# The last 512 columns of five weight stages, token-major like the rest

## The chip, the cores and the metric

The kernel runs on one core of a Trainium2 chip. The metric is the time of one execution on the device in microseconds (us). Three runs of the kernel before gave 1565.44 to 1566.68, median 1566.22. The engines are named as the profile names them: PE is TensorE (PEld its weight loads), DVE VectorE, ACT ScalarE, POOL GpSimd, and SP the queue from which nearly all loads are issued.

## What is computed

One layer over 256 tokens of width 2048, all in float32.

```
xn = rms_norm(x, norm_mix_g)
proj = xn @ w_in                        # 2048 -> 11264
u_s5, u_lru, q, k, v, gate_logits = split(proj)
g_s5, g_lru, g_attn = split(sigmoid(gate_logits + b_gate))      # 2048 each
y_s5   = s5_branch(u_s5)                # scan, gelu, gated by w_glu; width 1024
y_lru  = rglru_branch(u_lru)            # convolution, gates, scan; width 1024
y_attn = stick_breaking_attention(q, k, v)                      # 8 heads of 128
merged = g_s5*(y_s5 @ w_br_s5) + g_lru*(y_lru @ w_br_lru) + g_attn*(y_attn @ w_br_attn)
h = x + merged @ w_out                  # 2048 -> 2048
hidden = relu(rms_norm(h, norm_mlp_g) @ w_up) ** 2              # 2048 -> 8192
out = rms_norm(h + hidden @ w_down, final_norm_g)               # 8192 -> 2048
```

## The kernel before, in words

The work is one long stream of weights. Each weight matrix is cut into chunks of 512 output columns, and each chunk into units of two k-tiles (256 rows, 512 KB). Three buffers hold raw units, and three hold split units. A unit is loaded from SP's queue (L118), then split into two float32r parts: ACT casts it to `hi` (L134), and DVE subtracts to get `lo` (L135). The activations are split in the same way into a high and a low part, and each product is three matmuls: high by high, high by low, low by high. `next_unit` loads up to three units ahead and splits up to two ahead of the unit in use.

A chunk is computed in one of two ways. `chunk` (L196 to L198, tiles named mm_) holds 128 columns of the weights still and streams 256 tokens, so the result has channels on partitions: 12 matmuls of 256 columns for each k-tile. `chunk_tok` (L212 to L214, tiles named mt_) holds 128 tokens still and streams the 512 weight columns, so the result has tokens on partitions: 6 matmuls of 512 columns for each k-tile. Channel-major is the form that the next product needs as its input. A token-major result that the next product reads is brought over by `blocks`: 16 DVE transposes (L677), each a set of 32 by 32 blocks.

The stages, in order: parts of w_in; for lru and attn four times a gate chunk of w_in and a branch chunk; the same for s5, in the order g0, g1, w_glu twice, b0, g2, b1, b2, g3, b3; w_out (four chunks); then four rounds of w_up (four chunks of 512) and w_down (four chunks). In the gates, branches, w_out and each round of w_up the first three chunks are token-major and the fourth is channel-major. All of w_down is token-major.

Side work is written as generators. `later` puts one in a list with a rate, and `pump`, called after each unit's matmuls, takes that many steps from each. The S5 scan runs so beside the gates and attention. `split_tok` transposes 512 columns of the merged branches and splits them for w_out; `residual` transposes 512 columns of the residual `h_tok` into `hT` and splits them for w_up; `norm2` brings the last 512 columns of `hT` back to tokens with 16 transposes (L933), sums squares (L305, L309, L312) and ends in the PE matmuls `ps_n` (L923) and a few DVE steps; `hidden` transposes a chunk of relu(w_up), squares it on ACT and POOL (L987, L988) and splits it (L991) for w_down. Engines take their instructions in the order in which they are written, apart from small moves by a scheduler.

The lines that the change touches: in `gates` and `branch` the fourth chunk has its own code (L339, L702, L715 to L718). After the last s5 branch it is split at once (L852, L853). After w_out's fourth chunk the residual is added channel-major (L913) and split (L891, L892). After w_up's fourth chunk four instructions for each half make the split parts (L1013 to L1016). The residual input `xres` is loaded on ACT's queue (L878).

## Time and profile before

| | |
|---|---|
| median of three runs | 1566.22 us |
| profiled execution | 1565.52 us, its span 1563.8 us |
| PE busy | 1520.8 us (97%), 8430 matmuls |
| DVE busy | 1162.6 us (74%) |
| ACT busy | 807.9 us (52%) |
| POOL busy | 219.0 us (14%) |
| DMA | 291.78 MB, mean 187 GB/s |

The profile is one execution on the chip. Busy is the time in which an engine worked. Matmuls overlap each other in it, so the length of a stage and not the sum of its matmuls tells its cost. A row of the timeline shows start, duration, engine, line, operation, what it writes and reads, how many were merged, and in brackets the idle time before it with what ended that. A row of the stretches shows from:to, the length, the busy time of each engine with its count of instructions, the granted TensorE clock (1.00 is full), the busy share of the DMA engines and GB/s.

### The profile page before, as it was taken

To read this page: it belongs to the slowest core of one execution; us is meant where nothing else is said; L and a number is where in the kernel's file an instruction comes from. 1 tells how busy PE (TensorE), PEld (TensorE's weight loads), DVE (VectorE), ACT (ScalarE), POOL (GpSimd) and SP (SyncE) were. 2 spreads that over 40 slices of the span, in tenths; PEclk is the share of its full clock that TensorE was granted. 3 is DMA by queue.
4 is the path that set the end of the run, shared out by engine and by line. 5 is a ranking of instruction groups with operands and counts; after the bars stand their busy time and mean duration, and the time that the engine had idled before them with its cause. 6 is when DMAs were issued, how large, how long until landed. Compare 5 with 4: busy or idle time off the path is not lost.

```text
span 1563.8 us, 21927 instructions
## 1 busy us (share of the span) xinstructions
PE 1520.8 (97%) x8430; PEld 1316.4 (84%) x8430; DVE 1162.6 (74%) x1417; ACT 807.9 (52%) x976; POOL 219.0 (14%) x172
## 2 busy tenths in 40 slices
PE   9899999989999999999999999999999999999997
PEld 9897789978877788988889888888988898888986
DVE  5887998878979899578698895558655685558755
ACT  7468555486756555543444544344433444344443
POOL 5301113112112322101000010000100000000111
PEclk9999999999999999999999999999999999999999
DMA  9555665545536565655756556555566566655554
GB/s 282 156 169 172 188 197 174 176 135 168 178 115 199 172 188 176 205 192 167 279 191 194 183 167 197 194 193 191 189 194 196 189 190 192 196 190 192 191 196 148
DMA packets 88491, 291.78 MB, mean 187 GB/s; under 512 B 12738, under 2 KB 16962, under 8 KB 88130
## 3 DMA queue, kind: packets, MB, share of 16 engines
q1 hardware_dynamic: 87954, 287.14, 57.2%
q10 hardware_dynamic: 432, 3.24, 0.6%
q8 instruction: 66, 1.08, 0.3%
q14 instruction: 39, 0.32, 0.1%
HBM read 281.95 MB, written 2.10 MB: 182 GB/s over the span
## 4 chain that ended last, share of the span: by engine, by line
PE 80%; DVE 11%; ACT 4%; issue 3%; DMA 1%; DVEq 0%; ACTq 0%
PE mt_w_down L212 7%; PE mt_w_down L213 7%; PE mt_w_down L214 7%; PE mm_w_in L198 5%; PE mm_w_in L196 5%; PE mt_w_up L214 5%; PE mm_w_in L197 5%; PE mt_w_up L213 5%; PE mt_w_up L212 5%; DVE lo L135 4%; PE mt_w_in L213 3%; PE mt_w_in L214 3%; PE mt_w_in L212 3%; PE mm_w_up L198 2%; PE mm_w_up L197 2%
## 5 line engine op out<-in xcount | busy, mean ns | idle before, releaser
L135 DVE TENSOR_TENSOR lo<-raw,hi 128x1024 fp32r<-128x1024 f32 (+1 forms) x521 | 660.9, 1272 | 327.6 <-ACT hi L134 323.0
L134 ACT CAST hi<-raw 128x1024 fp32r<-128x1024 f32 (+1 forms) x521 | 545.3, 1049 | 661.2 <-PE mt_w_down L214 197.6
L198 PE MATMUL mm_w_in<-xhi,lo 128*128 128x256 f32 x704 | 202.1, 288 | 7.3 <-DVE lo L135 7.3
L196 PE MATMUL mm_w_in<-xhi,hi 128*128 128x256 f32 x704 | 202.4, 288 | 1.8 <-DVE rs L297 1.2
L213 PE MATMUL mt_w_down<-lo,hd_hi 128*128 128x512 f32 (+1 forms) x528 | 202.1, 383 | 0.0
L212 PE MATMUL mt_w_down<-hi,hd_hi 128*128 128x512 f32 (+1 forms) x528 | 202.1, 383 | 0.0
L214 PE MATMUL mt_w_down<-hi,hd_lo 128*128 128x512 f32 (+1 forms) x528 | 202.0, 383 | 0.0
L197 PE MATMUL mm_w_in<-xlo,hi 128*128 128x256 f32 x704 | 201.3, 286 | 0.0
L213 PE MATMUL mt_w_up<-lo,hhi 128*128 128x512 f32 x384 | 150.0, 391 | 2.5 <-DVE lo L135 2.5
L214 PE MATMUL mt_w_up<-hi,hlo 128*128 128x512 f32 x384 | 149.5, 389 | 0.0
L212 PE MATMUL mt_w_up<-hi,hhi 128*128 128x512 f32 x384 | 149.4, 389 | 0.0
L213 PE MATMUL mt_w_in<-lo,xhi 128*128 128x512 f32 x352 | 140.8, 400 | 7.5 <-DVE lo L135 7.3
L212 PE MATMUL mt_w_in<-hi,xhi 128*128 128x512 f32 x352 | 141.4, 403 | 3.9 <-ACT hi L134 3.9
L198 PEld LDWEIGHTS mm_w_in<-xhi,lo 128*128 128x128 f32 x704 | 136.9, 195 | 9.5 <-DVE lo L135 9.1
L196 PEld LDWEIGHTS mm_w_in<-xhi,hi 128*128 128x128 f32 x704 | 137.3, 195 | 4.1 <-issue 2.6
L214 PE MATMUL mt_w_in<-hi,xlo 128*128 128x512 f32 x352 | 139.4, 396 | 0.0
L197 PEld LDWEIGHTS mm_w_in<-xlo,hi 128*128 128x128 f32 x704 | 137.3, 195 | 0.2
L214 PEld LDWEIGHTS mt_w_down<-hi,hd_lo 128*128 128x128 f32 x528 | 99.2, 188 | 19.4
L212 PEld LDWEIGHTS mt_w_down<-hi,hd_hi 128*128 128x128 f32 x528 | 99.2, 188 | 19.3
L213 PEld LDWEIGHTS mt_w_down<-lo,hd_hi 128*128 128x128 f32 x528 | 99.2, 188 | 19.2
L988 POOL TENSOR_TENSOR reluT<-reluT 128x1024 f32<-128x1024 f32 x12 | 23.8, 1984 | 642.9 <-ACT hd_hi L987 519.5
L213 PEld LDWEIGHTS mt_w_up<-lo,hhi 128*128 128x128 f32 x384 | 72.1, 188 | 19.3 <-DVE lo L135 4.5
(328 smaller groups left out, 2600.0 us busy)
## 6 DMA issues: line engine op xcount, KB each, us to landing
raw<-in_w_in SPq DMA_DIRECT2D x175, 512.0 KB, 3.6
raw<-in_w_up SPq DMA_DIRECT2D x128, 512.0 KB, 3.4
raw<-in_w_down SPq DMA_DIRECT2D x128, 512.0 KB, 4.1
raw<-in_w_out SPq DMA_DIRECT2D x32, 512.0 KB, 4.3
raw<-in_w_br_lru SPq DMA_DIRECT2D x16, 512.0 KB, 3.8
raw<-in_w_br_attn SPq DMA_DIRECT2D x16, 512.0 KB, 3.5
raw<-in_w_br_s SPq DMA_DIRECT2D x16, 512.0 KB, 3.5
stk<-ux SPq DMA_DIRECT2D x96, 64.0 KB, 3.3
```

The lines of the kernel that those rows point to most:

```text
L134: anchor["act"] = nc.scalar.copy(h[:, k, :], r[:, k, :]).ins
L135: anchor["dve"] = nc.vector.tensor_tensor(l_[:, k, :], r[:, k, :], h[:, k, :].bitcast(F32), ALU.subtract).ins
L196: nc.tensor.matmul(o, wh[:, kk, s], xh, start=first and ct % 2 == 0, stop=False, skip_group_check=True)
L197: nc.tensor.matmul(o, wh[:, kk, s], xl, start=False, stop=False, skip_group_check=True)
L198: mm = nc.tensor.matmul(o, wl[:, kk, s], xh, start=False, stop=last and ct % 2 == 1, skip_group_check=True)
L212: nc.tensor.matmul(banks[j], xh[:, s], wh[:, a:b], start=kt == 0, stop=False)
L213: nc.tensor.matmul(banks[j], xh[:, s], wl[:, a:b], start=False, stop=False)
L214: return nc.tensor.matmul(banks[j], xl[:, s], wh[:, a:b], start=False, stop=kt == ng * UK - 1)
L988: nc.gpsimd.tensor_tensor(rT, rT, rT, ALU.mult)
```

## The change

The fourth chunk of the gates, of the branch outputs, of w_out and of each round of w_up is computed by `chunk_tok` like the other three. `m_tok` and `x_tok` now hold all 2048 columns. The last columns are transposed by side work at a rate of 2.0 steps a unit under the next stage's first chunk, and the next stage's k-tiles 12 to 15, which are the ones that come from these columns, call `finish` on that side work. `norm2` no longer transposes back to tokens, and starts when the last `residual` is done. `mT3`, the transposed last columns of the branches, lies in the buffer of `reluT`. The gate's bias row is loaded for the fourth chunk too, as one more DMA on SP for each of the three branches, and the channel-major bias leaves the parameter block.

```diff
     def gates(idx, c, alloc):
-        if c < 3:
-            gb = tmp.tile([P, CH], F32, tag="gbias", name=f"gb{idx}_{c}", bufs=1)
-            ...
-        banks = (chunk_tok if c < 3 else chunk)("w_in", GATE0 + 4 * idx + c, D, xs)
+        gb = tmp.tile([P, CH], F32, tag="gbias", name=f"gb{idx}_{c}", bufs=1)
+        o = idx * D + c * CH
+        nc.sync.dma_start(gb, repeat(io["b_gate_row"][:, o:o + CH], P))
+        banks = chunk_tok("w_in", GATE0 + 4 * idx + c, D, xs)
         gts = []
         for j in range(2):
-            ...
+            g = alloc(c, j).rearrange("p a l -> p (a l)")
+            nc.vector.scalar_tensor_tensor(g, banks[j], rstd_tok[:, j:j + 1], gb, ALU.mult, ALU.add)
+            nc.scalar.activation(g, g, AF.Sigmoid)
             gts.append(g)
         return gts
 
-    def branch(idx, c, gts, wname, ys, split=None):
-        ...
+    def branch(idx, c, gts, wname, ys):
+        banks = chunk_tok(wname, c, W, ys)
         for j in range(2):
-            ...
+            m, g = m_tok[:, j, c * CH:(c + 1) * CH], gts[j]
+            if idx == 1:
+                nc.vector.tensor_tensor(m, banks[j], g, ALU.mult)
             else:
-                ...
+                nc.vector.tensor_tensor(g, banks[j], g, ALU.mult)
                 nc.gpsimd.tensor_tensor(m, m, g, ALU.add)
...
-    def split_tok(c):
-        mT = pp.tile([P, 4, L], F32, tag="v", name=f"mT{c}")
+    def split_tok(c, mT):
         yield
         yield from blocks(m_tok[:, :, c * CH:(c + 1) * CH], mT, 4)
         split_pair(4 * c, 4, mT)
...
+    last = later([split_tok(3, mlp.tile([P, 4, L], F32, tag="reluT", name="mT3", bufs=2))], 2.0)
...
     def ms(kt):
+        if kt >= 12:
+            finish(last)
         h_, l_ = mg[kt // 8]
         return h_[:, kt % 8, :], l_[:, kt % 8, :]
...
-    for c in range(3):
+    for c in range(4):
         banks = chunk_tok("w_out", c, D, ms)
         s = slice(c * CH, (c + 1) * CH)
         for t in range(2):
             nc.vector.tensor_tensor(h_tok[:, t, s], banks[t], x_tok[:, t, s], ALU.add)
-        rq = later([residual(c)], 1.0)
-    banks = chunk("w_out", 3, D, ms)
-    finish(rq)
-    ...
+        rq = later([residual(c)], 2.0 if c == 3 else 1.0)
+
+    def hs(kt):
+        if kt >= 12:
+            finish(rq)
+        return hhi[:, kt, :], hlo[:, kt, :]
 
     def norm2():
-        yield from to_tokens()
+        while rq[0]:
+            yield
         yield from square_sum(hT)
...
-            last = c == FQ // CH - 1
-            banks = (chunk if last else chunk_tok)("w_up", q * (FQ // CH) + c, D, lambda kt: (hhi[:, kt, :], hlo[:, kt, :]))
+            banks = chunk_tok("w_up", q * (FQ // CH) + c, D, hs)
...
-            for j in range(2):
-                ...
+            r = mlp.tile([P, 2, CH], F32, tag="relu", name=f"relu{q}_{c}", bufs=2)
+            for t in range(2):
+                nc.scalar.activation(r[:, t, :], banks[t], AF.Relu)
+            k = slice((c % 2) * 4, (c % 2) * 4 + 4)
+            hq = later([hidden(r, h_[:, k, :], l_[:, k, :], f"{q}_{c}")], 2.0 if c == FQ // CH - 1 else 1.0)
 
         def hs_(kt):
+            if kt >= 12:
+                finish(hq)
             h_, l_ = hd[kt // 8]
             return h_[:, kt % 8, :], l_[:, kt % 8, :]
```

How this moves instructions is seen in VectorE's order at three places. The rows show line, operation, output and inputs, shape and count; the numbers behind lo, hi and raw only tell units apart. First the passage from the first round's w_up to w_down. Before, from the split of the unit ahead of w_down's first to the fifth split behind it:

```order
L135 TENSOR_TENSOR lo_8856<-raw_8822,hi_8855 128x1024
L1016 TENSOR_TENSOR hd_lo_2_8617<-relu_3_0_8883,hd_hi_2_8616 128x512
L135 TENSOR_TENSOR lo_8898<-raw_8853,hi_8897 128x1024
L1016 TENSOR_TENSOR hd_lo_2_8617<-relu_3_1_8888,hd_hi_2_8616 128x512
L135 TENSOR_TENSOR lo_8916<-raw_8895,hi_8915 128x1024
L135 TENSOR_TENSOR lo_8934<-raw_8913,hi_8933 128x1024
```

Now, the same passage. Its first row is the split of w_down's unit 1, the second that of unit 2:

```order
L135 TENSOR_TENSOR lo_8259<-raw_8237,hi_8258 128x1024
L135 TENSOR_TENSOR lo_8282<-raw_8256,hi_8281 128x1024
L677 STREAM_TRANSPOSE reluT_3_8297<-relu_3_8274 32x2x4x32 x8
L135 TENSOR_TENSOR lo_8309<-raw_8279,hi_8308 128x1024
L677 STREAM_TRANSPOSE reluT_3_8297<-relu_3_8274 32x2x4x32 x8
L135 TENSOR_TENSOR lo_8335<-raw_8306,hi_8334 128x1024
L135 TENSOR_TENSOR lo_8355<-raw_8332,hi_8354 128x1024
L966 TENSOR_TENSOR hd_lo_2_8104<-reluT_3_8297,hd_hi_2_8103 128x1024
```

Two splits of 512 columns have gone; sixteen transposes in two groups and one split of 1024 have come, behind the splits of units 2, 3 and 5.

The second place is the passage from the last s5 branch chunk to w_out, after the two products with the gate. Before:

```order
L717 TENSOR_TENSOR gate_3_1_7175<-mm_w_br_s_3_1_228_7180,gate_3_1_7175 128x512
L135 TENSOR_TENSOR lo_7327<-raw_7271,hi_7326 128x1024
L853 TENSOR_TENSOR mg_ylo_7108<-mT_6938,mg_yhi_7107 128x1024
L853 TENSOR_TENSOR mg_ylo_7108<-merged,mg_yhi_7107 128x512 x2
L135 TENSOR_TENSOR lo_7345<-raw_7324,hi_7344 128x1024
```

Now:

```order
L704 TENSOR_TENSOR gate_3_1_6792<-mt_w_br_s_3_1_228_6796,gate_3_1_6792 128x512
L838 TENSOR_TENSOR mg_ylo_6750<-mT_6614,mg_yhi_6749 128x1024
L135 TENSOR_TENSOR lo_6892<-raw_6851,hi_6891 128x1024
L677 STREAM_TRANSPOSE mT_6881<-merged 32x2x4x32 x4
L135 TENSOR_TENSOR lo_6914<-raw_6889,hi_6913 128x1024
L677 STREAM_TRANSPOSE mT_6881<-merged 32x2x4x32 x8
L135 TENSOR_TENSOR lo_6940<-raw_6911,hi_6939 128x1024
L677 STREAM_TRANSPOSE mT_6881<-merged 32x2x4x32 x4
L135 TENSOR_TENSOR lo_6964<-raw_6937,hi_6963 128x1024
L135 TENSOR_TENSOR lo_6982<-raw_6961,hi_6981 128x1024
L838 TENSOR_TENSOR mg_ylo_6750<-mT_6881,mg_yhi_6749 128x1024
```

The split of the last columns has moved behind that of w_out's unit 6, with sixteen transposes ahead of it.

The third place is the first round's first chunk of w_up, now, from its unit 2 on:

```order
L135 TENSOR_TENSOR lo_7579<-raw_7549,hi_7578 128x1024
L677 STREAM_TRANSPOSE hT<-h_tok 32x2x4x32 x4
L135 TENSOR_TENSOR lo_7601<-raw_7576,hi_7600 128x1024
L677 STREAM_TRANSPOSE hT<-h_tok 32x2x4x32 x8
L135 TENSOR_TENSOR lo_7627<-raw_7598,hi_7626 128x1024
L677 STREAM_TRANSPOSE hT<-h_tok 32x2x4x32 x4
L135 TENSOR_TENSOR lo_7653<-raw_7624,hi_7652 128x1024
L876 SCALAR_TENSOR_TENSOR hlo<-hT,par,hhi 128x256 x4
L135 TENSOR_TENSOR lo_7677<-raw_7650,hi_7676 128x1024
L135 TENSOR_TENSOR lo_7697<-raw_7674,hi_7696 128x1024
L309 TENSOR_TENSOR hT<-hT 128x1024
```

Before, one transpose back to tokens (L933) stood behind each split here, and the first sum of squares (L309) came in the third chunk.

## The prediction

> **What bounds the kernel now.** I read the page first, its parts 1 and 4.

> ```profile
> PE 1520.8 (97%) x8430; PEld 1316.4 (84%) x8430; DVE 1162.6 (74%) x1417; ACT 807.9 (52%) x976; POOL 219.0 (14%) x172
> ...
> PE 80%; DVE 11%; ACT 4%; issue 3%; DMA 1%; DVEq 0%; ACTq 0%
> ```

> TensorE is busy for 97% of the span, but 11% of the chain that ended last runs over VectorE. So matmul time counts where VectorE keeps up, and VectorE time counts elsewhere. Next the stretches by stage: from:to, length, then busy time (instructions) of PE, PEld, DVE, ACT, POOL, the clock, the DMA share, GB/s.

> ```profile
> 824.20:847.40 23.20, 23.20 (x194) 23.15 (x193) 19.92 (x32) 10.11 (x12) 0.00 (x0) 1.00 0.62 194
> 1028.20:1093.50 65.30, 65.30 (x290) 54.07 (x289) 48.11 (x60) 29.68 (x31) 3.79 (x2) 1.00 0.57 187
> 1093.50:1116.60 23.10, 23.10 (x194) 23.06 (x193) 19.01 (x26) 10.53 (x12) 1.89 (x1) 1.00 0.62 200
> 1116.60:1138.40 21.80, 21.80 (x99) 18.08 (x98) 11.12 (x11) 10.14 (x12) 2.89 (x2) 1.00 0.60 193
> 847.40:918.10 70.70, 67.29 (x294) 53.95 (x294) 61.28 (x85) 36.30 (x41) 4.87 (x2) 1.00 0.55 175
> 228.40:266.00 37.60, 37.16 (x302) 35.70 (x300) 31.92 (x34) 20.73 (x26) 13.28 (x9) 1.00 0.59 188
> 560.20:600.20 40.00, 38.53 (x310) 36.37 (x308) 38.83 (x43) 22.17 (x28) 11.34 (x7) 1.00 0.56 175
> 722.90:747.40 24.50, 23.75 (x193) 23.23 (x192) 23.60 (x37) 9.24 (x9) 3.54 (x2) 1.00 0.47 153
> 747.40:758.90 11.50, 11.50 (x98) 11.50 (x97) 6.50 (x8) 5.69 (x8) 0.00 (x0) 1.00 0.69 229
> ```

> The second row is three token-major chunks of w_up: 65.30 us, 21.77 each, 2.72 for each of a chunk's eight units. The third row is the channel-major fourth chunk, 23.10; the first is that of w_out, 23.20. The fourth row, w_down's first chunk, has no gap and VectorE only half busy. The fifth row is the first round of w_up: 5.4 over the 65.3 of the next round. The last four rows are the channel-major gate and branch chunks (lru, attn, and the s5 gate and branch apart).

> **The change part by part.** Units count from 0, times from the start of the stage's first matmul; lo(4) is the VectorE part of unit 4's split.

> *TensorE.* A token-major chunk costs 21.77 (10.9 for the branches' eight k-tiles). The four chunks of w_up save 23.10 - 21.77 = 1.33 each, **-5.3**; w_out's saves **-1.4**. Both had idle time on VectorE, and the neighbouring token-major chunks run without a gap, so all of it is on the path. [...]

> *w_up to w_down, four times.* The chunk's transposes now come eight to a unit into VectorE's queue behind w_down's lo(2) and lo(3). Before, two short splits stood there. Here are rows of the same work in the first round, where five transposes stood between two splits, and in the s5 gate, where eight did (start, duration, engine, line).

> ```profile
> 868.77 1.28 ACT L1005 ACTIVATE relu<-mt_w_up 128x512 f32<-128x512 f32 x2 [0.98 <-PE mt_w_up L214]
> 869.94 1.04 ACT L134 CAST hi<-raw 128x1024 fp32r<-128x1024 f32 x1
> 871.02 1.23 DVE L135 TENSOR_TENSOR lo<-raw,hi 128x1024 fp32r<-128x1024 f32 x1 [1.50 <-ACT hi L134]
> 872.72 1.78 DVE L677 STREAM_TRANSPOSE reluT<-relu 32x256 f32<-32x256 f32 x4
> 874.53 1.23 DVE L135 TENSOR_TENSOR lo<-raw,hi 128x1024 fp32r<-128x1024 f32 x1
> 885.10 1.23 DVE L135 TENSOR_TENSOR lo<-raw,hi 128x1024 fp32r<-128x1024 f32 x1
> 886.38 0.50 PE L213 MATMUL mt_w_up<-lo,hhi 128*128 128x512 f32 x1 [0.43 <-DVE lo L135]
> 733.76 3.57 DVE L677 STREAM_TRANSPOSE mT<-merged 32x256 f32<-32x256 f32 x8
> 737.36 1.23 DVE L135 TENSOR_TENSOR lo<-raw,hi 128x1024 fp32r<-128x1024 f32 x1
> 738.64 0.39 PE L198 MATMUL mm_w_in<-xhi,lo 128*128 128x256 f32 x1 [0.74 <-DVE lo L135]
> ```

> The second matmul of a unit waits for its lo and starts 0.05 after it. In that chunk (start 869.1) lo(2) starts at 1.9, behind two relus and a cast on ScalarE. From there: lo(2) to 3.15, eight transposes (3.57) to 6.75, lo(3) to 8.0 (needed at 3 x 2.72 + 0.23 = 8.4), eight transposes to 11.6, lo(4) to 12.85, needed at 11.1. TensorE waits 1.8. Behind it in VectorE's queue stand lo(5) and hd_lo; after the pause lo(5) has 2.5 us more, hd_lo ends about 16.2 and unit 6, the first to read it, starts at 18.2. So 1.8 x 4 = **+7.2**. Bounds: 0 if the pieces found free slots, 2 x 1.8 if the late lo also delays the raw tile that takes its buffer.

> *s5 branch to w_out.* Transposes 4, 8, 4 of `mT3` now follow lo(2), lo(3), lo(4). The first group waits for the two GpSimd additions into `merged`.

> ```profile
> 759.37 3.54 POOL L718 TENSOR_TENSOR merged<-merged,gate 128x512 f32<-128x512 f32 x2 [29.73 <-DVE gate L717]
> 761.67 2.31 DVE L853 TENSOR_TENSOR mg_ylo<-mT,mg_yhi 128x1024 fp32r<-128x1024 f32 x1
> 773.21 1.05 ACT L134 CAST hi<-raw 128x1024 fp32r<-128x1024 f32 x1 [4.72 <-DMA raw<-in_w_out]
> ```

> The start was 758.9: the additions end at 4.0, and the older split of `mT` (2.31 beside GpSimd) at 3.6. lo(2) to 4.9, four transposes to 6.7, lo(3) 7.9, eight 11.5, lo(4) 12.7 against 11.1 (1.6 late), four 14.5, lo(5) 15.7 against 15.5: 1.6 + 0.2 = **+1.8**. The x_res transfer, which already held back raw tiles here (third row), comes at the same time as before. On ScalarE the wait for the additions is now that transfer's and no longer the cast's; hi(3) stands behind it and is ready at 5.5. Bounds 0 and 3.5.

> *w_out to w_up, first round.* The sixteen transposes back to tokens go; sixteen of `hT` come, with the residual's splits, and norm2 then follows in the first chunk and not in the third.

> ```profile
> 848.50 1.71 ACT L891 ACTIVATE hhi<-hT,par 128x256 fp32r<-128x256 f32 x4
> 849.77 1.67 DVE L892 SCALAR_TENSOR_TENSOR hlo<-hT,par,hhi 128x256 fp32r<-128x256 f32 x4
> 893.62 2.00 ACT L305 ACTIVATE hT<-hT 128x1024 f32<-128x1024 f32 x2
> 909.93 1.22 DVE L312 TENSOR_TENSOR hT<-hT 128x1024 f32<-128x1024 f32 x1
> 913.91 0.68 DVE L312 TENSOR_TENSOR hT<-hT 128x512 f32<-128x512 f32 x1
> 915.65 0.41 DVE L312 TENSOR_TENSOR hT<-hT 128x256 f32<-128x256 f32 x1
> 916.12 0.60 PE L923 MATMUL ps_n<-ones,hT 128*128 128x1 f32 x4 [0.89 <-DVE hT L312]
> ```

> Carried along the queues from lo(2), which follows two additions and ends at 2.75: four transposes to 4.55, lo(3) 5.8, eight 9.4, lo(4) 10.6, four 12.4, so that lo(5) ends at 13.65 (needed 13.8), the four hhi on ScalarE at 14.2, the hlo at 15.4, lo(6) at 16.8 against 16.55, and with two more squares ahead of its cast lo(7) at 19.8 against 19.6: 0.6 lost. The hT sums stand between the next chunk's splits; the last ends at 28.5, and in TensorE's order ps_n stands after the seventh matmul of that chunk's second unit, at 26.7: 1.8 lost, and some 0.6 for ps_n and a late split. 3.0 in place of 5.4: **-2.4**, bounds +1 and -5.4.

> *Gates and branches.* TensorE needs 1.33 + 0.6 less in each of three places; VectorE needs as much as before there (the extra transposes are counted above). With VectorE busy for 31.92 of 37.60 I take 0.8 of the 1.9; with 38.83 of 40.00, 0.4; in the s5 gate (23.60 of 24.50) 0.1, since the eight transposes above set its pace, and in the branch behind it (6.50 of 11.50) all 0.6. **-1.9**, bounds 0 and -5.8. Three more 256 KB bias rows pass SP's queue ahead of raw loads, as nine did; nothing on TensorE waits for them now.

> Sum: -5.3 - 1.4 + 7.2 + 1.8 - 2.4 - 1.9 = -2.0. The profiled execution took 1565.52 (span 1563.8), so 1563.5; the median of the runs is 0.7 above it, 1566.22, and so **1564.2**.

> **Rivals.** (a) *The transposes are hidden*: VectorE is half idle in w_down's first chunk (11.12 of 21.80), and by unit 6 there is time enough. Then the +7.2 and +1.8 fall away: 1555.2, or 1559.7 with half of them. Against it: the rows at 733.76 to 738.64 show eight transposes in one go already costing 0.74. (b) *Slower through the clock.* In a pause the granted clock can fall.

> ```profile
> 282.81 0.38 PE L198 MATMUL mm_w_in<-xhi,lo 128*128 128x256 f32 x1 [1.90 <-DVE lo L135]
> 283.60:286.80 3.20, 3.20 (x17) 3.20 (x16) 1.43 (x2) 0.00 (x0) 0.00 (x0) 0.51 0.88 244
> 500.54 0.50 PE L213 MATMUL mt_w_in<-lo,xhi 128*128 128x512 f32 x1 [1.51 <-DVE lo L135]
> 500.60:504.00 3.40, 3.40 (x15) 2.78 (x16) 3.40 (x5) 0.66 (x1) 0.00 (x0) 1.00 0.68 205
> ```

> An idle time of 1.90 was followed by 3.2 us at a clock of 0.51; one of 1.51 by none (clock 1.00). A wait of 1.8 shows as an idle time of some 1.65, since a matmul's record runs on past the point where the next could start (the row at 886.38: 0.6 late, 0.43 idle); that lies between the two. Decided the bad way, each of the four stops costs 1.6 more: +6.4, 1570.6. [...] (c) *The ring of three buffers*: a late lo frees its raw tile late, the load lands late, and a second stop follows in each w_down, another 7.2: 1571.4. Against it: in the rows from 871.02 to 886.38 five splits in a row came late, and TensorE stopped once. (d) The chunks do not get shorter because VectorE paces them: only in the early stages, which the bounds above hold.

> **How the numbers follow.** This kernel's measurement tells about 0.2% (3.1 us) from no change: faster is below 1563.1, slower above 1569.3. The forecast gets 0.59, with its own range of 1562 to 1566.5 from the bounds of the early stages and norm2; a quarter of it (0.15) lies below 1563.1. (a) gets 0.24, all faster; (b) 0.11 and (c) 0.06, slower. So 0.39 faster, 0.44 same, 0.17 slower. The range takes in the half-hidden form of (a) and most of the way to (b): 1559 to 1569.

> **What would show it.** Chunks of w_up at 21.8 in all four places; in each w_down's first chunk one wait of some 1.8 at its fifth unit, for lo, with clock 1.00; w_down's other chunks unchanged; in w_out's first chunk one or two waits together 1.9; the first round of w_up at 68 for its three chunks. No wait at w_down's fifth unit speaks for (a), a clock of 0.5 behind it for (b), a second wait with a DMA as releaser for (c). The forecast is wrong if the waits do not follow the groups of eight.

## The result: 0.23% slower

The changed kernel takes 1569.13 us (median of 20 runs, 1565.38 to 1575.49), the kernel before 1565.41 (20 runs beside them, 1563.45 to 1567.70). The ratio is 1.0023, with a 95% interval of 1.0014 to 1.0031. The prediction said 1564.2, a gain of 2.0; what came is a loss of 3.7, just outside the range. Two later measurements of the changed kernel gave 1.0021 (1.0008 to 1.0034) and, with one harmless addition (e6), 1.0025 (1.0014 to 1.0035). Three disturbed executions, one of e3 (3058 us) and two of the kernel before beside e5 to e8 (1664 and 1858 us), are left out of all figures.

The profiled execution of the changed kernel is the shortest of its 20 runs: 1565.38, span 1563.7. Its page, busy times and the chain of work that ended last:

```profile
PE 1509.8 (97%) x7518; PEld 1264.0 (81%) x7518; DVE 1194.2 (76%) x1492; ACT 806.2 (52%) x965; POOL 216.8 (14%) x168
...
PE 62%; DVE 20%; ACT 6%; issue 6%; DMA 5%; SPq 0%; DVEq 0%; ACTq 0%
```

TensorE needs 11 us less, and that is what the change was to bring. But the share of the chain that runs over VectorE went from 11% to 20%, and loads, 1% before, hold 5% of it. Matmul time went down and waits came in its place. Where they are, the stretches by stage show (from:to, length, then busy time and instructions of PE, PEld, DVE, ACT, POOL, granted clock, DMA share, GB/s):

```profile
228.00:264.70 36.70, 35.26 (x156) 27.57 (x155) 32.02 (x34) 20.31 (x24) 12.96 (x9) 1.00 0.63 197
557.20:597.00 39.80, 37.88 (x169) 28.25 (x167) 39.00 (x43) 21.36 (x25) 11.62 (x7) 1.00 0.58 175
719.20:743.50 24.30, 22.92 (x97) 17.71 (x96) 22.89 (x36) 9.25 (x9) 3.53 (x2) 1.00 0.48 152
743.50:754.40 10.90, 10.90 (x49) 9.02 (x49) 6.98 (x8) 5.15 (x6) 0.00 (x0) 1.00 0.80 239
754.40:845.00 90.60, 88.06 (x385) 71.86 (x384) 79.51 (x120) 40.25 (x46) 3.54 (x2) 1.00 0.68 219
845.00:933.80 88.80, 87.87 (x390) 72.47 (x389) 79.80 (x115) 46.94 (x52) 5.69 (x3) 1.00 0.61 189
933.80:1023.30 89.50, 87.56 (x385) 71.90 (x384) 50.87 (x56) 35.59 (x35) 2.91 (x1) 1.00 0.61 191
1023.30:1110.40 87.10, 87.10 (x386) 72.12 (x385) 67.01 (x86) 40.14 (x42) 5.69 (x3) 1.00 0.62 189
1110.40:1200.40 90.00, 87.65 (x386) 71.91 (x385) 50.89 (x56) 35.59 (x35) 2.91 (x1) 1.00 0.63 192
1287.40:1377.10 89.70, 87.68 (x385) 71.92 (x384) 50.96 (x57) 35.66 (x35) 2.91 (x1) 1.00 0.61 191
1464.20:1555.20 91.00, 88.51 (x434) 74.46 (x432) 55.81 (x68) 39.40 (x52) 14.82 (x8) 1.00 0.53 167
```

In order: the last gate and branch of lru, of attn, the last s5 gate, its branch; w_out; w_up and w_down of round one; w_up of round two (as in rounds three and four); w_down of rounds two, three and four. Every w_up chunk now takes 21.76, and a round of w_up 87.0 where it took 88.4. The four w_down stages took 87.0, 87.0, 87.0 and 87.9 before; now 89.6, 90.0, 89.7 and 91.1, which is 11.6 more in all. w_out is 90.6 after 88.4.

This is how one w_down stage begins, by the chain of waits (start, duration, what). The stage starts at 1110.4.

```profile
1104.82 2.16 DVE lo L135
...
1106.99 5.50 DMA raw<-in_w_down
...
1112.57 1.06 ACT hi L134
...
1113.65 1.23 DVE lo L135
1114.88 0.34 DVE reluT L677
...
1118.40 1.22 DVE lo L135
...
1119.65 0.43 DVE reluT L677
...
1123.27 1.24 DVE lo L135
...
1124.55 0.50 PE mt_w_down L213
```

From lo(2) on this is the queue that the prediction carried forward: lo and eight transposes are 4.75 and then 4.87 us, while TensorE needs a unit every 2.72. Two things differ. The chain does not start at the relu but earlier, at a lo that took 2.16 beside GpSimd's square of the previous chunk; it freed a raw tile late, and the load into that tile took 5.50. So lo(2) begins 3.3 into the chunk, not 1.9. And TensorE waits twice (the idle time stands in brackets):

```profile
1119.67 0.50 PE L213 MATMUL mt_w_down<-lo,hd_hi 128*128 128x512 f32 x1 [0.53 <-DVE lo L135]
1124.55 0.50 PE L213 MATMUL mt_w_down<-lo,hd_hi 128*128 128x512 f32 x1 [1.82 <-DVE lo L135]
```

By the spacing of its weight loads the matmul stream loses 0.91 at the first, in front of unit 3, and 2.21 at the second, in front of unit 4. In the four rounds the first wait is 0.46, 0.91, 0.56 and 1.03, the second 2.25, 2.21, 2.23 and 2.23.

### The profile page after: what moved, and what is told of

The parts are those of the page before. It is cut to its first block, busy times and chain, and to the rows that moved or that the text cites. A ratio compares the mean times of both kernels' runs of the same rounds, so it can differ in the third digit from the quotient of the medians.

```text
span 1563.7 us, 20155 instructions
## 1 busy us (share of the span) xinstructions
PE 1509.8 (97%) x7518; PEld 1264.0 (81%) x7518; DVE 1194.2 (76%) x1492; ACT 806.2 (52%) x965; POOL 216.8 (14%) x168
## 4 chain that ended last, share of the span: by engine, by line
PE 62%; DVE 20%; ACT 6%; issue 6%; DMA 5%; SPq 0%; DVEq 0%; ACTq 0%
DVE lo L135 7%; PE mt_w_down L213 6%; PE mt_w_down L214 6%; PE mt_w_down L212 6%; PE mt_w_up L213 5%; PE mt_w_up L214 5%; PE mt_w_up L212 5%; DVE reluT L677 3%; DMA raw<-in_w_in 3%; PE mt_w_in L213 3%; ACT hi L134 3%; PE mt_w_in L214 3%; PE mt_w_in L212 3%; PE mm_w_in L196 3%; PE mm_w_in L198 3%
## 5 line engine op out<-in xcount | busy, mean ns | idle before, releaser
L135 DVE TENSOR_TENSOR lo<-raw,hi 128x1024 fp32r<-128x1024 f32 (+1 forms) x521 | 660.9, 1274 | 304.2 <-ACT hi L134 301.3
L134 ACT CAST hi<-raw 128x1024 fp32r<-128x1024 f32 (+1 forms) x521 | 545.3, 1049 | 649.7 <-PE mt_w_down L214 162.6
L213 PE MATMUL mt_w_down<-lo,hd_hi 128*128 128x512 f32 (+1 forms) x528 | 203.0, 385 | 8.8 <-DVE lo L135 8.7
L214 PE MATMUL mt_w_down<-hi,hd_lo 128*128 128x512 f32 (+1 forms) x528 | 202.1, 383 | 0.0
L213 PE MATMUL mt_w_up<-lo,hhi 128*128 128x512 f32 x512 | 199.3, 389 | 0.0
L212 PE MATMUL mt_w_up<-hi,hhi 128*128 128x512 f32 x512 | 199.2, 389 | 0.0
L214 PE MATMUL mt_w_up<-hi,hlo 128*128 128x512 f32 x512 | 199.2, 389 | 0.0
L213 PE MATMUL mt_w_in<-lo,xhi 128*128 128x512 f32 x448 | 179.4, 400 | 11.8 <-DVE lo L135 11.7
L214 PE MATMUL mt_w_in<-hi,xlo 128*128 128x512 f32 x448 | 176.9, 395 | 0.0
L198 PE MATMUL mm_w_in<-xhi,lo 128*128 128x256 f32 x512 | 146.3, 287 | 4.8 <-DVE lo L135 4.8
L196 PE MATMUL mm_w_in<-xhi,hi 128*128 128x256 f32 x512 | 146.9, 287 | 2.7 <-ACT hi L134 1.8
L197 PE MATMUL mm_w_in<-xlo,hi 128*128 128x256 f32 x512 | 145.9, 285 | 0.0
L213 PEld LDWEIGHTS mt_w_down<-lo,hd_hi 128*128 128x128 f32 x528 | 99.2, 188 | 31.3 <-DVE lo L135 12.2
L212 PEld LDWEIGHTS mt_w_down<-hi,hd_hi 128*128 128x128 f32 x528 | 99.2, 188 | 19.6
L213 PEld LDWEIGHTS mt_w_in<-lo,xhi 128*128 128x128 f32 x448 | 85.4, 191 | 36.4 <-DVE lo L135 19.1
L214 PEld LDWEIGHTS mt_w_down<-hi,hd_lo 128*128 128x128 f32 x528 | 99.2, 188 | 19.2
L677 DVE STREAM_TRANSPOSE reluT<-relu 32x256 f32<-32x256 f32 x256 | 111.5, 436 | 4.1
L212 PEld LDWEIGHTS mt_w_up<-hi,hhi 128*128 128x128 f32 x512 | 96.1, 188 | 20.1
L213 PEld LDWEIGHTS mt_w_up<-lo,hhi 128*128 128x128 f32 x512 | 96.1, 188 | 20.0
```

What stands on the lines that cost most here:

```text
L134: anchor["act"] = nc.scalar.copy(h[:, k, :], r[:, k, :]).ins
L135: anchor["dve"] = nc.vector.tensor_tensor(l_[:, k, :], r[:, k, :], h[:, k, :].bitcast(F32), ALU.subtract).ins
L196: nc.tensor.matmul(o, wh[:, kk, s], xh, start=first and ct % 2 == 0, stop=False, skip_group_check=True)
L197: nc.tensor.matmul(o, wh[:, kk, s], xl, start=False, stop=False, skip_group_check=True)
L198: mm = nc.tensor.matmul(o, wl[:, kk, s], xh, start=False, stop=last and ct % 2 == 1, skip_group_check=True)
L212: nc.tensor.matmul(banks[j], xh[:, s], wh[:, a:b], start=kt == 0, stop=False)
```

## The experiments

The stops are read off the stream of TensorE's weight loads: its regular pitch is 0.227 us, and a stop is what a gap has beyond it. "Length" of a stage, and a time "into" it, count from its first weight load (0.1 to 0.2 ahead of its first matmul) to the next stage's first.

The first question was why the median of 20 runs lies 3.7 above the profiled execution. Each run lists the mean clock that TensorE was granted: the run of 1575.5 had 0.988, three of 1570.4 to 1572.0 had 0.989, nine of 1568.8 to 1570.9 had 0.990, and the seven up to 1568.2 had 0.991 to 0.993. In the traces the granted clock falls to 0.50 for stretches of 3.41 us (6.83 once in the first profile); half of 3.41 is 1.7 us, by which one such stretch lowers the mean by an estimated 0.0011. That is rival (b) of the prediction, and the first experiments were chosen by it.

**e1: the last chunk of w_up put back.** Round for round the code of the kernel before stands in w_up's fourth chunk:

```diff
-            banks = chunk_tok("w_up", q * (FQ // CH) + c, D, hs)
+            last = c == FQ // CH - 1
+            banks = (chunk if last else chunk_tok)("w_up", q * (FQ // CH) + c, D, hs)
...
-            if kt >= 12:
-                finish(hq)
```

> The change with one part undone: the last 512 columns of w_up channel-major again in all four rounds, so that w_down's first chunk has no transposes beside it; gates, branches and w_out stay token-major. From the changed kernel's profiled execution (1565.4): the four w_down stops go (2.6 + 3.1 + 2.4 + 3.3 = 11.4, read as the length of each w_down round over the 87.0 it has without a stop) and four chunks of w_up cost 1.4 more each (5.5): 1559.5. Theory (the stops cost their own length, and a stop that falls inside one 3.41 us clock window halves the clock of the next, 1.7 more): only w_out's stop is left, so the median is 1560 to 1561 and the runs spread by less than 5. Rival (the clock has nothing to do with the stops, and the 3.7 by which the changed kernel's median lies over its profiled execution come from elsewhere): 1563, with a spread as wide as the changed kernel's 10.

Measured: 1563.05 (1560.87 to 1565.01), ratio to the kernel before 0.9987 (0.9977 to 0.9997). No stop is left in w_down:

```profile
939.40:1026.40 87.00, 87.00 (x387) 72.07 (x386) 44.40 (x41) 35.51 (x36) 2.89 (x2) 1.00 0.60 194
```

From w_out's start to w_down's end it takes 795.2, the first profile of the changed kernel 800.8: 5.6 less, where 11.4 - 5.5 = 5.9 was expected. The spread is 4.1. The median is 2 above the expectation, because the latter was counted from an execution whose early stages had been short (w_out starts at 754.4 there, at 758.6 here, with the same instructions ahead of it). So by these lengths the w_up part of the change loses 5.6, and the other parts together gain 2.0 against the kernel before. On the clock this run does not decide.

**e2: the last chunk of w_up alone.** The kernel before with only that part of the change: `chunk_tok` for every chunk of w_up, `hidden` of the last at rate 2.0, and `finish(hq)` from the thirteenth k-tile of w_down on.

> The kernel before with one part of the change: only w_up's last chunk of each round token-major, its transposes at rate 2 under w_down's first chunk. Saved 4 x 1.4 = 5.5, stops of 11.4: +5.9 over the kernel before, 1571.3, if the stops cost only their length. Theory with the clock: four more stops of which somewhat over half fall inside one window, about 2.2 x 1.7 = 3.7 on top: 1575, runs spread by 6 to 10. The prediction's own sizes (5.3 saved, 7.2 of stops) would give 1567.3.

Measured: 1566.08 (1562.72 to 1569.13), ratio 1.0014 (1.0003 to 1.0026). One row of its w_down stages, and the wait in it:

```profile
1111.80:1200.60 88.80, 87.40 (x386) 72.05 (x385) 51.28 (x57) 35.55 (x35) 2.92 (x1) 1.00 0.60 193
```

```profile
1124.70 0.50 PE L213 MATMUL mt_w_down<-lo,hd_hi 128*128 128x512 f32 x1 [1.40 <-DVE lo L135]
```

All four rounds stop once, for 1.79, 1.78, 1.79 and 1.79. This is the prediction's size, and the expectation of 11.4 was the one that missed. The order of instructions in these stages is the changed kernel's; what differs is that lo(2) begins 2.0 into the chunk and not 3.3, since the load that its cast needs has landed. And 1.40 of idle in one place brought no half clock; the prediction had put the idle time of such a stop at 1.65.

**e3: TensorE kept busy in the stops.** Ahead of unit 4 of w_down's and w_out's first chunk stand matmuls into a bank that nobody reads, and in rounds two to four three more ahead of unit 3:

```diff
+                if n:
+                    idle = pss.tile([P, CH], F32, tag="ps", name=f"idle_{name}_{st['use']}")
+                    for _ in range(n):
+                        nc.tensor.matmul(idle, src[:, 0, 0:P], src[:, 0:2, :].rearrange("p a l -> p (a l)"), start=True, stop=True, skip_group_check=True)
...
+fill=(hd[0][0], {4: 8} if q == 0 else {3: 3, 4: 8})
```

> The changed kernel with matmuls of no use put where PE stops: 8 of 512 columns (8 x 0.227 = 1.8 us) ahead of the fifth unit of w_down's first chunk in every round and of w_out's first chunk, and 3 (0.7 us) ahead of the fourth unit in rounds two to four. Nobody reads what they write. They lie in the 2.2 us stops, so the stops keep their length, and PE is no longer idle in them. Theory (idle PE halves the clock of the next window): no half clock after 600 us in any run, median 1565 to 1566.5, 2.5 to 4 below the changed kernel's 1569.1, spread under 5. Rival (the clock's windows do not come from the stops): median 1569 to 1571 and the spread of 10 stays.

Measured: 1566.67 (1565.04 to 1568.64), ratio 1.0017 (1.0008 to 1.0026). The spread is 3.6 as the theory wanted, the median is 0.2 above its range, and against the changed kernel's 1.0023 the intervals overlap. Its profile can't be compared by stages. Not decided.

**e4: the same transposes, spread.** Four ahead of w_down's first unit, four behind each of the next three; the square that GpSimd took goes to ScalarE for this chunk.

```diff
-            hq = later([hidden(r, h_[:, k, :], l_[:, k, :], f"{q}_{c}")], 2.0 if c == FQ // CH - 1 else 1.0)
+            hq = later([hidden(r, h_[:, k, :], l_[:, k, :], f"{q}_{c}", c == FQ // CH - 1)], 1.0)
+            if c == FQ // CH - 1:
+                step(hq)
...
+        if due:
+            nc.scalar.activation(rT, rT, AF.Square)
```

> The changed kernel with the same transposes in w_down's first chunk spread: four ahead of its first unit and four behind each of the next three, in place of eight behind the first and eight behind the second; for this chunk the square that POOL took is on ACT. Theory (eight transposes and a lo subtract, 4.9 us, do not fit a unit of 2.72, four and a subtract, 3.0, nearly do): lo(4) is in time, at most 0.8 of a wait at the seventh unit, where the last chunk's hidden values are read; the 11.4 of stops shrink to 0 to 3: 1554 to 1557 by the profiled execution, median 1555 to 1558. Rival (16 transposes in this chunk are too many for DVE wherever they stand): the stop moves to the seventh unit at its old size, 1565 to 1569.

Measured: 1560.29 (1557.63 to 1564.34), ratio 0.9972 (0.9961 to 0.9983). The wait at unit 4 is gone; one of 0.9 at the seventh unit has come, for hd_lo, with 0.4 and 0.8 more in the last two rounds: 4.8 in all in place of 11.6. hi(6) stood behind both squares on ScalarE. Two things differ here from the changed kernel, the places of the transposes and the engine of one square; e12 parts them. Both runs say that not the number of transposes makes the stop at the fifth unit but how they stand in the queue.

**e5: the changed kernel again**, unaltered, since its loads had landed later than those of e2.

> The changed kernel itself, unaltered, beside the other three of this group. In its first profile the weight loads landed later than in the kernel before (w_in 4.1 us in the median against 3.6, w_up 4.0 against 3.4), from the first stage on, where no instruction differs; w_down's stops came to 11.4, whereas e2, whose loads land as before (3.5 and 3.3), stopped for 1.79 a round, 7.2. If the slow loads belong to the kernel: again 4.0 to 4.1, stops of w_down of 10 to 12, 2 to 4 us over the kernel before. If they belong to that one execution: 3.4 to 3.6, stops of about 7.5, and within 1 us of the kernel before.

Measured: 1567.90 (1562.80 to 1571.77), ratio 1.0021 (1.0008 to 1.0034). Loads at 4.2 (w_in) and 4.0 (w_up); the w_down stages 89.55, 89.49, 88.75 and 90.74, that is 9.8 over those of before. Three rounds stop for 2.24 with 0.37 to 0.69 ahead; the third stops once, for 1.78, and there no load was late. The long form is the kernel's own, but not in every round.

**e6: the tile of parameters as large as before.** The 48 columns of b_gate are kept in `par`, loaded and not read.

```diff
-PAR = {"norm_mix_g": 16, "norm_mlp_g": 16, "s5_d": 8,
+PAR = {"norm_mix_g": 16, "norm_mlp_g": 16, "b_gate": 48, "s5_d": 8,
```

> The changed kernel with one thing put back that it need not have: the 48 columns of b_gate in the packed input par and its tile (192 bytes of each partition), loaded and read by nobody, so that what is allotted behind it lies where it lay before; not an instruction moves. If the place of the buffers makes the loads slow: landing 3.4 to 3.6 again, w_down's stops 1.8 a round (7 to 8 in all), w_out's 2 to 3, and the time 4 to 6 us below e5. If it does not: 4.0, and within 1.5 us of e5.

Measured: 1568.20 (1566.77 to 1570.62), ratio 1.0025 (1.0014 to 1.0035), loads at 4.2 and 4.0, as in e5: the place of what lies behind `par` is acquitted. But its profile caught what the first one had not. Windows of the clock, round one and round two:

```profile
946.55:949.96 3.41, 1.59 (x7) 1.01 (x6) 3.33 (x7) 1.53 (x2) 0.34 (x1) 1.00 0.27 103
949.96:953.38 3.42, 3.42 (x9) 2.64 (x9) 1.64 (x2) 0.46 (x1) 2.58 (x1) 0.50 0.67 202
...
1124.04:1127.45 3.41, 1.65 (x8) 1.03 (x6) 3.32 (x7) 1.17 (x2) 0.00 (x0) 1.00 0.35 135
1127.45:1130.87 3.42, 3.32 (x14) 2.74 (x15) 1.63 (x3) 0.82 (x1) 2.91 (x1) 1.00 0.60 193
```

PE's busy time is the first number behind the length. With 1.59 busy, 1.82 idle, the next window has the clock at 0.50 and takes 9 matmuls; with 1.65 busy, 1.76 idle, it stays at 1.00. The stages with such a window, rounds one and three, took 91.1 and 91.2, the second one 89.3: 1.9 apart.

**e7: only the fifth unit filled**, eight matmuls in each of the five stops.

> As e3, but with the useless matmuls only ahead of the fifth unit (8 of 512 columns, 1.8 us, in w_down's first chunk of each round and in w_out's), where the stop is in every profile of the changed kernel; e3's own profile was of a disturbed execution. Theory (a window of 3.41 us in which PE idles 1.6 or more is followed by one at half the clock, 1.7 us): the idle of these stops falls under 0.6, no half clock after 760 us; the time is 1.5 to 4 below e5, with a smaller spread. Rival: e5's median within 1, spread as e5's. Should the stop be only 1.8 in a fast execution, the filling costs nothing or 0.1 each.

Measured: 1563.54 (1559.45 to 1566.91), ratio 0.9995 (0.9985 to 1.0006), against e5's 1567.90 beside it: 4.4 less, and the two intervals do not touch. Two of its w_down stages:

```profile
1111.50:1200.30 88.80, 88.80 (x393) 73.53 (x392) 51.57 (x57) 35.36 (x35) 2.91 (x1) 1.00 0.61 193
...
1287.30:1376.20 88.90, 88.90 (x394) 73.58 (x393) 50.98 (x57) 35.45 (x35) 2.91 (x1) 1.00 0.61 193
```

PE is busy for the whole length, and after 760 us no window has a halved clock; but e5's one profile has none there either. In the two profiles w_out and the four w_downs together differ by 1.0 (8.3 + 1.6 over the stages of before against 9.8 + 1.1). More work, done in vain, came with a faster kernel, as the theory wanted, but it doesn't show that the clock is the reason. The mean granted clock of the runs is 0.9920 against e5's 0.9912 (each run's is given to three places), which is some 1.2 us; e6's is 0.9903, and against it 2.7. And something else went: in rounds two to four the load for lo(2) took 3.5 to 3.6 here and not 5.0, so that w_down starts as in e2. How the 4.4 divides between the clock and the load is not shown.

**e8: a version without the stops.** Gates and branches as before, w_out's last chunk as in the change, w_up's last chunk token-major and spread as in e4, with both squares one unit later, behind hi(6):

```diff
+        if due:
+            yield
         nc.scalar.activation(h_, rT, AF.Square)
-        nc.gpsimd.tensor_tensor(rT, rT, rT, ALU.mult)
-        yield
-        yield
+        if due:
+            nc.scalar.activation(rT, rT, AF.Square)
```

> A version to beat both: gates and branches as before (no transposes under w_out's first chunk); w_out's last chunk token-major with its transposes under w_up, as in the change; w_up's last chunk token-major with the transposes in w_down's first chunk spread as in e4, and both squares of that chunk one unit later, behind hi(6) (in e4 hi(6) stood behind them on ACT, and lo(6) and hd_lo were 0.9 late). From the stage lengths: w_out 1.4 less, w_up of round one 5.1 less (its 70.7 + 23.1 became 88.8), the three other rounds 1.4 less each, w_down at its 87.0 of before if no stop is left: 10.6 below the kernel before, 1554 to 1556. If the wait at the seventh unit stays as in e4 (0.9 to 1.4): 1558 to 1560. If the 16 transposes cannot be hidden (e2's 1.8): 1562.

Measured: 1558.06 (1557.25 to 1558.50, five runs), ratio 0.9960 (0.9948 to 0.9972): 0.4% under the kernel before and 0.6% under the changed one. VectorE's queue at the start of a w_down (stage start 1111.3), and the stage:

```profile
1112.33 1.78 DVE L677 STREAM_TRANSPOSE reluT<-relu 32x256 f32<-32x256 f32 x4 [1.04 <-ACT relu L997]
1114.14 1.23 DVE L135 TENSOR_TENSOR lo<-raw,hi 128x1024 fp32r<-128x1024 f32 x1
1115.40 1.79 DVE L677 STREAM_TRANSPOSE reluT<-relu 32x256 f32<-32x256 f32 x4
1117.21 1.23 DVE L135 TENSOR_TENSOR lo<-raw,hi 128x1024 fp32r<-128x1024 f32 x1
...
1123.37 2.36 DVE L135 TENSOR_TENSOR lo<-raw,hi 128x1024 fp32r<-128x1024 f32 x2
1125.78 1.23 DVE L985 TENSOR_TENSOR hd_lo<-reluT,hd_hi 128x1024 fp32r<-128x1024 f32 x1
```

```profile
1111.30:1198.30 87.00, 87.00 (x385) 72.04 (x384) 51.19 (x56) 36.34 (x36) 0.00 (x0) 1.00 0.62 197
```

Four transposes and a lo take 3.07 against the unit's 2.72, so VectorE falls back 0.35 a unit, which its lead bears; hd_lo is done at 15.7, before unit 6 starts at 16.3. The same sixteen transposes, and no stop in any w_down, though w_up's and w_in's loads took 4.2 and 4.3 here. The median is 2 above the expectation; w_out starts at 760.4 in its profile, 1.5 later than in the profile of before, and waits once for a load (0.8).

**e9: the kernel before, again**, for its loads.

> The kernel before, unaltered, for its weight loads. Its first profile and e2's had w_in at 3.5 to 3.6 us and w_up at 3.3 to 3.4 from issue to landing; seven profiles of the changed kernel and its variants had 4.1 to 4.3 and 3.9 to 4.2, with par as before too (e6), and in the first stage, where no instruction differs. If the slower loads belong to the changed kernels: 3.6 and 3.4 here. If they belong to the execution or to where the program was loaded: they may be 4.1 and 4.0 here as well, at a time within 0.3% of the kernel before all the same.

Measured: 1564.49, loads at 3.5 (w_in) and 3.3 (w_up). In these profiles the slower loads go with the changed kernels.

**e10: w_out's last chunk alone**: `chunk_tok` for all four chunks of w_out, `residual(3)` at rate 2.0 under w_up, norm2 as in the change, everything else as before.

> The kernel before with one part of the change: w_out's last chunk token-major, its four blocks of transposes under w_up's first chunk at rate 2, the second norm waiting for them and its 16 single transposes gone. Gates, branches and w_up's last chunks as before. By the stage lengths: w_out 88.4 to 87.0 or 87.7, w_up of round one 93.9 to 66.9 + 23.1 = 90.1: 4.5 to 5.2 below the kernel before, 1559.5 to 1560.5. The prediction's sizes for this part (w_out 1.4, the stalls of w_up's round one 5.4 to 3.0) give 3.8 less, 1561. Rival (its transposes at 8 a unit stop w_up's second half of the first chunk as they stop w_down's): 1.8 to 2.2 more than that, 1562 to 1563.

Measured: 1559.91 (1555.88 to 1563.02), ratio 0.9975 (0.9966 to 0.9984): 4.0 less. w_up of round one is 67.00 + 23.14 after 70.72 + 23.14, w_out 87.62 after 88.42. This part of the change is all gain; its eight transposes in one unit cost nothing in w_up. The one stop left there is the norm's, 1.76; w_out waits once, 0.74.

**e11: the whole change, both late stages spread.** As e8 in w_down; in w_out's first chunk four transposes a unit, and the last branch's additions on VectorE.

```diff
-                nc.gpsimd.tensor_tensor(m, m, g, ALU.add)
+                (nc.vector if idx == 0 and c == 3 else nc.gpsimd).tensor_tensor(m, m, g, ALU.add)
...
-    last = later([split_tok(3, ...)], 2.0)
+    last = later([split_tok(3, ...)], 1.0)
```

> The whole change with both late stages relieved: w_down's first chunk as in e8; in w_out's first chunk four transposes a unit from the first unit on instead of four, eight and four, the last branch's two adds on DVE in place of POOL (POOL's 3.5 us slow the lo subtract beside it from 1.23 to 2.3). Against e8 it has gates and branches token-major (1.7 less by the stage lengths) and the transposes under w_out. If w_out's first chunk then stops for 1.5: 1558, level with e8. If the last chunk's split, which cannot start before the sixteenth transpose, comes late at the seventh unit instead: a wait of 2 to 3 there, 1559 to 1560. If the 2.7 to 3.8 of the changed kernel stay: 1560 to 1561.

Measured: 1559.87 (1557.94 to 1562.47), ratio 0.9977 (0.9968 to 0.9986). w_down's stages are 87.04, 87.05, 87.06 and 87.97, without a stop again, although the load for lo(2) was late in all four rounds (4.7 to 5.6). But w_out takes 91.35, longer than with groups of eight. Its longest wait:

```profile
782.48 0.73 PE L212 MATMUL mt_w_out<-hi,mg_yhi 128*128 128x512 f32 x2 [1.98 <-ACT hi L134]
```

There the transposes can't start at once: they need the sum of all three branches, and the older split stands ahead of them. Spread, the sixteenth transpose ends at 778.2, 17.3 into a chunk that wants the split at 16.3, and the split itself is done at 781.7. This wait runs 0.8 beyond it, to a cast whose load was late: by the order of the rows the scheduler put the first matmul of unit 8 ahead of those that read the split. Two stops at the sixth unit (0.67 and 1.03) belong to another load, which took 8.4 beside the x_res transfer. So the stop moved and did not shrink, and loads add to it.

**e12: rate 1 for the hidden values** in the changed kernel, nothing else:

```diff
-..., f"{q}_{c}")], 2.0 if c == FQ // CH - 1 else 1.0)
+..., f"{q}_{c}")], 1.0)
```

> The changed kernel with one number altered: the last chunk's hidden values at rate 1 in place of 2 (four transposes a unit from the first unit's end, as under the other chunks), POOL's square kept. Theory (what DVE has beside a unit decides where the stop is): no stop at the fifth unit; the sixteenth transpose ends at about 14.4 us into the chunk as under w_up, ACT, POOL and the subtract follow, hd_lo is there at 19 to 20, wanted at 16.5: one stop of 2.5 to 4 at the seventh unit in each round, 10 to 16 in all against the 10 to 11 of the changed kernel: 1568 to 1573. Rival (rate 2 was the whole fault): no stop, 1558.

Measured: 1572.46 (1566.83 to 1573.39, four runs), ratio 1.0047 (1.0031 to 1.0063). The fifth unit is free, and each round stops at the seventh for 2.3 to 2.9. Two of the four rounds by windows of the clock, and the wait of the first:

```profile
1134.56 0.50 PE L214 MATMUL mt_w_down<-hi,hd_lo 128*128 128x512 f32 x1 [2.25 <-DVE hd_lo L966]
```

```profile
1131.60:1135.01 3.41, 1.16 (x6) 0.65 (x5) 1.74 (x2) 1.49 (x2) 1.64 (x1) 1.00 0.55 154
1135.01:1138.43 3.42, 3.42 (x10) 2.63 (x9) 1.76 (x2) 0.00 (x0) 0.00 (x0) 0.50 0.47 150
...
1486.59:1490.00 3.41, 2.16 (x10) 1.47 (x8) 1.50 (x2) 2.81 (x3) 1.90 (x1) 1.00 0.56 186
1490.00:1493.41 3.41, 2.65 (x11) 2.17 (x12) 2.98 (x3) 0.03 (x1) 0.00 (x0) 1.00 0.32 77
```

Nearly the same stop, 2.63 and 2.39: the one lies in a single window (2.25 idle) and halves the next, the other is cut by a window's edge into 1.25 and 0.76 and halves none. The first three rounds took 4.0 to 4.2 more than before, the fourth 2.4.

**e13, e14, e15: a longer program.** The four profiles with fast loads had the most matmuls. One-column matmuls of no use were put behind the last one, so that nothing ahead of them moves; their time at the end (1785, 1947 and 1768 in all) means nothing.

```diff
+    more = pss.tile([P, CH], F32, tag="ps", name="more")
+    for _ in range(528):
+        nc.tensor.matmul(more[:, 0:1], ones, ones[:, 0:1], start=True, stop=True, skip_group_check=True)
```

> The changed kernel with 528 one-column matmuls of no use behind its last one, so that TensorE's program has as many matmuls as e2's (8046 in place of 7518); nothing ahead of them moves. Four profiles with 8046 or more matmuls (kernel before twice, e2, e10) had w_in's loads at 3.4 to 3.6 us, nine with 7950 or fewer at 4.1 to 4.3. If the length of the program (and with it the place of what is loaded behind it) sets that: w_in 3.4 to 3.6, w_up 3.3 to 3.4 here, and if late loads made the stops longer than e2's, w_down's first chunks stop for 1.8 each, 7.2 in all, without a wait at the fourth unit. If not: 4.1 and 4.0 and stops of 10 to 14. The program's end comes some 30 to 80 us later and says nothing; the stage lengths are read.

> As e13 with 912, as many matmuls as the kernel before (8430). By the length of the program: 3.4 to 3.6 and 3.3 to 3.4, stops of 1.8. Otherwise 4.1 and 4.0. If e13 and e14 differ, it is not a length from which on the loads are fast, but where each length puts things.

> e8 with the same 528 matmuls behind its end (8478): its w_in loads took 4.3 and w_up's 4.2. By the length of the program 3.4 to 3.6 here. Its stages had no stop in w_down at 4.3 and should have none at 3.4; w_out's 0.8 (a wait for a load beside the x_res transfer) may go.

The loads of the changed kernel, by the page's part on DMA issues (count, size, median us to landing), and then those of e13:

```profile
raw<-in_w_in SPq DMA_DIRECT2D x175, 512.0 KB, 4.1
raw<-in_w_up SPq DMA_DIRECT2D x128, 512.0 KB, 4.0
```

```profile
raw<-in_w_in SPq DMA_DIRECT2D x175, 512.0 KB, 3.7
raw<-in_w_up SPq DMA_DIRECT2D x128, 512.0 KB, 3.4
```

e14 has 3.8 and 3.5, e15 3.5 and 3.4. So the loads differ with what stands behind the end of the program, but not by a plain rule of its length: in the first stage alone (5 to 110 us) they are at 3.5 in e13 and e15 and at 4.3 in e14, the longest of the three. The added matmuls count double in the traces, so there are 8574, 9342 and 9006. But the stops did not follow: e13's second waits are 2.25, 2.23, 2.26 and 2.25, and its w_down stages 14.1 over those of before, e14's 14.4. The theory that the slower loads in general make the longer stops has fallen. Late is one load in particular: issued 3.4 before the stage starts, in e13 it takes 5.2, and the two ahead of it 3.2 and 3.4. In e2 the load in that place takes 3.2 and the one behind it 4.4. These two are issued 1.2 apart, because the slow lo holds back the raw tile of the first.

The traces show something beside the late load. They hold sixteen completions for a load. In the late loads fifteen have come after 3.1 to 3.8 us, and one comes 0.7 to 2.3 later (in the four rounds of the first profile 1.46, 1.96, 1.44 and 2.09): a single part of the sixteen is behind. The pages have a queue named instruction (packets, MB, share), first for the kernel before, then for the changed one:

```profile
q8 instruction: 66, 1.08, 0.3%
q8 instruction: 59, 0.97, 0.3%
```

Each of these packets has 16 KB. There are 66 for 16942 instructions of TensorE (16860 of them matmuls and weight loads) and 59 for 15124 (15036), one for some 256 each time; between two packets lie 222 to 300 matmuls and weight loads in the one profile and 219 to 291 in the other. So the packets keep step with TensorE's instructions; what is in them the traces don't say. In 33 rounds (of the first profile, e4 to e7 and e11 to e14) such a packet begins 1.0 to 3.0 us behind the issue of that load, and in 32 of them the load takes 4.45 to 5.80. In fifteen rounds (e2, e8, e15 and three of e7) none begins there, and it takes 3.1 to 3.7. A round of the changed kernel has 1536 matmuls and weight loads, six times 256, and all four rounds are hit alike: in the first profile the packet begins 1.89, 1.78, 1.97 and 2.52 behind the load's issue. In e2, whose program ahead of these stages is another, the packet falls on the load before (4.25 to 4.8 there), which has time to spare. In e7 each round has sixteen instructions more, and from the second round on the packet begins ahead of the load's issue, and the load is in time.

## Why the prediction was wrong

Its terms one by one, in us against the stages of before, for the first profile, e5 and e6:

| term | predicted | first | e5 | e6 |
|---|---|---|---|---|
| w_up, rounds two to four | -4.0 | -4.1 | -4.1 | -4.1 |
| w_up, round one (chunk and norm) | -3.7 | -5.1 | -5.1 | -5.2 |
| w_out (chunk and the stop) | +0.4 | +2.2 | +1.1 | +1.0 |
| w_down, four stops | +7.2 | +11.6 | +9.8 | +13.8 |

**Gates and branches** went nearly as predicted: in the first profile -0.59, -0.22, -0.20 and -0.64 by the weight loads, together -1.65 (predicted -0.8, -0.4, -0.1 and -0.6). **The token-major chunk** is worth 1.38 by the weight loads and 1.27 by the matmuls (predicted 1.33); the 0.11 between them stands in w_down's row. **Norm2** gained more than predicted: one wait of 1.73 for ps_n is left, and the 0.6 ahead of it and the 0.6 behind it did not come. **w_out**: the waits at units 4 and 5 are 1.85 and 0.68, not 1.6 and 0.2. The row for lo(2) was taken as 1.23; it took 2.31 beside GpSimd's additions, which the neighbouring row of mg_ylo had shown. In the first profile a late load added 0.24 and 1.03. That norm2's error and w_out's partly cancel is luck.

**The step that failed is the four stops of w_down, 1.8 x 4.** Their place, cause and count are as predicted, and alone (e2) they are of the predicted size to 0.02. With the rest of the change they are not. Over the first profile, e5, e6, e13 and e14, twenty rounds, the term is 12.7 and not 7.2, and 5.5 more is nearly the 5.7 between the change that was forecast (-2.0) and the one measured (+3.7). It was missed twice:

- *The start.* lo(2) was timed from the relu. That holds where its load has landed (2.0 into the chunk in e2), but in 19 of the twenty rounds the load took 4.6 to 5.6, lo(2) waited for it, and the stop at unit 4 is 2.17 to 2.26 long; in the one round with a load of 3.5 it is 1.78. Thirteen of the twenty rounds have no half clock; they take 2.65 longer on average, not 1.8: +3.4 over four rounds. The previous chunk's lo, 2.15 beside GpSimd's square where the median of the rest is 1.23, is as slow in e2 and puts the load's issue in the same place; it leaves the load little time, and with an instruction packet beside it the load took 4.45 to 5.80 in 32 of 33 rounds, without one 3.1 to 3.7 in fifteen. The four rounds of e2, which show the predicted size, are among the fifteen. So there is a late load, as in rival (c), but it comes ahead of the stop and is not made by it, and it costs 0.85 a round, not 1.8.
- *The clock.* Seven of the twenty rounds have a halved window and take 4.17 longer, 1.5 more: +2.1 over four rounds. That is rival (b), whose price of 1.6 was about right. Its condition was weighed for a stop of 1.8 alone, and no margin was left for a longer one. The rounds of one profile show it (e6: 91.1 and 91.2 with a halved window, 89.3 without, some 0.4 of that their first wait). e7 agrees, but there the load was in time as well.

The 1.90 of rival (b)'s row was no lower bound: in e6 1.82 of idle time in a window was followed by the half clock.

**Rival (a)**, transposes hidden, was right in principle and wrong for this code: e8 hides all of them in w_down. The argument against it, eight in one go costing 0.74, was an argument against groups of eight.

*Not settled.* One round in which an instruction packet fell on the load and the load was not late (e5's third) is unexplained, and no run moved the packets alone: e7 did so together with its matmuls. Why loads in general differ with what stands behind the program's end (w_in at 4.1 in the changed kernel, 3.7 in e13, 3.8 in e14) is open too. A fourth raw buffer, which would part the load from the stop, was not tried. And the medians of the changed kernel lie 3.5 to 3.8 above before, while the terms above and the -1.7 of gates and branches (from the first profile) sum to +2.9, 0.0 and +3.8; the rest is at most the size of two halved windows; the early stages have some in every profile, the kernel before's too.

## What to carry to other kernels

Work that is put under another stage must fit unit by unit, not over the stage: VectorE was half idle in w_down's first chunk, and groups of 4.8 us against a unit of 2.72 still stopped TensorE; the same work started at once, four to a unit and with both squares on ScalarE behind the casts, cost nothing (87.00 in e8, as before). Four to a unit alone did not do it (e12). Where the moved work could not start at once because its input was late (w_out here), spreading it only moved the stop (91.35 in e11 after 90.6). And a queue's start should be read from the stage ahead of it, from its slowest instruction and the load that this holds back, with the longest time that such a load takes in the trace (5.50 here) and not the usual one (3.5), before a stop is given a size.

## What the runs showed of the hardware

The queue that the profile names instruction moved packets of 16 KB, one for some 256 matmuls and weight loads (59 for 15124 instructions of TensorE in the changed kernel). Where such a packet began 1.0 to 3.0 us behind the issue of a 512 KB load, at the place looked at, the last of the load's sixteen completions came 0.7 to 2.3 us after the other fifteen, in 32 of 33 cases.

The weight loads of one and the same first stage (5 to 110 us) took 3.7 to 3.8 in the kernel before and e2, and 4.2 to 4.4 in the first profile, e5, e6, e7 and e8, with no instruction different there; 528 matmuls added behind the end of the program brought 3.5, 912 left 4.3.
